# Four units of r: columns two ahead, splits a product earlier, Silu as one pass per row, the fourth unit's sums in memory

## The chip, the cores and the metric

One core of a Trainium2 chip runs the whole program. The metric is the device time of one execution in microseconds (us); lower is better. The engines are named as in the profile: PE (TensorE, the matmuls), ACT (ScalarE), DVE (VectorE), POOL (GpSimd), and SP (SyncE), which issues the DMAs. Each engine takes its instructions in the order in which they were written into its queue.

## The reference

One layer of an encoder trunk over 1024 tokens of width 1024, in float32. What matters here, cut:

```python
h = rmsnorm(x, norm_mix)
q, k, v, r, lr_f, lr_b, u, g_a, g_b = split(h @ w_in)
# four heads: a gated linear attention over chunks, forward scan plus backward scan
o = gla_chunked(q, k, v, log_a_f) + flip(gla_chunked(flip(q), flip(k), flip(v), flip(log_a_b)))
o = o * rsqrt(mean(o * o) + EPS) * gla_norm
o = o * silu(r)                       # r: 1024 x 1024, the product h @ w_in[:, r columns]
y_a = o @ w_branch_gla
y_b = pooled(u) @ w_pool_group * pool_scale
x = x + (sigmoid(g_a) * y_a + sigmoid(g_b) * y_b) @ w_out
x = x + (silu(gate) * up) @ w_ffn_out      # gate, up = split(rmsnorm(x) @ w_ffn_in)
return rmsnorm(x, norm_final)
```

## The kernel before, in words

**Numbers and products.** A float32 operand is split into a high and a low part (`split_to`, L200): ACT casts the high part (`wh`, `trh`, `kt`, `p`, L201 or L689), then POOL (for weights, `wl`, L202) or DVE (for activations, `trl` L693, `kt`, `p`) subtracts it from the operand for the low part. A product takes three matmuls: high by high, low by high, high by low. The big projections use a seven-product scheme for a 2 x 2 block of a matrix product: products p = 1 to 7, each of a sum of weight blocks with a sum of blocks of h. Products 1, 2 and 4 take weight blocks as they lie in memory, 3, 5, 6 and 7 take sums of blocks; on the side of h, products 4 to 7 take sums ("feature sums", held in memory as `f_out`, loaded by `load_sums` into `trl`, cast by `cast_sum` into `trh`, and made low by `low_sum`).

**Units of r.** The columns of r fall into four units of 256 (u = 0 to 3; TRIO = 3). Units 0 to 2 are the r stage: 21 products in the order `R_PRODUCTS` by unit, with weights that are loaded by `r_load` (tiles `rr`, from `w_in` for p = 1, 2, 4 and from `r_out` for the sums) and split by `r_split`. `r_out` is filled early: `r_jobs` (L642) loads a unit's two column tiles (`rraw`), has POOL form four sums of them (L742), and stores them (L723). These jobs run beside the attention of the second and third heads, one step at a time (`beside`, L713; `prepare_beside`), and `finish_beside` ends what is left in head 3's projection. Unit 3 is handled as unit 0 of the stage after (`gunits`, `gate_runs`, `Gates`): its sums are formed by DVE (`fs`, L1189) from two loaded column tiles (`fraw`), ahead of use by `Ahead`.

**What runs beside it.** `attention(h)` is a generator that is advanced in small steps between the matmuls of whatever PE projects (`pump`, L166, takes the time passed; `soon` puts a step off by a delay). In the r stage that is the attention of head 3. Its state goes through `advance` (L972): PE makes kv, DVE the new state `st`, ACT two scaled copies, `sf` or `sb` for PE and `so` for the next state; forward chunks use sf, backward chunks sb. `scores` (L992) masks by a DVE copy (L1002), and splits the result into p for PE. At the head's end the output is normed and turned, and stored to `o_out` (L563).

**Order around the change.** `project_qk(3)` (L852) calls, ahead of k's products, `finish_beside`, the load of the feature sums for p = 5 and the loads of the first four r weights; after each half of k it splits one. In the r stage each product n loads weight n + 5 and splits n + 3, and then runs the steps of `r_events` (L1337): loads and casts of feature sums two or three products ahead of use, the loads of `o_out` (`ol`), and `gate_row`. `r_evict` (L1323) takes a bank out of PSUM: the first product of a quarter is copied, later ones are added by DVE, and the last one goes through Silu on ACT, in halves of 512 columns. `gate_row` multiplies a row of r by o.

Of the kernel before, what the change touches and what calls it, by code (L numbers as in the profile page):

```python
# [10 lines left out]
F32 = mybir.dt.float32  # L11
# [43 lines left out]
def kernel(  # L55
# [583 lines left out]
    TRIO = KT // 2 - 1  # L639
    r_out = [{p: dram.tile([P, 4, P], F32, name=f"r_out{u}_{p}") for p in (3, 5, 6, 7)} for u in range(TRIO)]  # L640

    def r_jobs(u):  # L642
        raw = [slot(F32, (KT, P), "rraw")[:, :, :] for _ in range(2)]
        a11, a12, a21, a22 = (t[:, 4 * j : 4 * j + 4, :] for t in raw for j in range(2))
        yield from loading(
            [w_in[:, c0 : c0 + P].rearrange("(k p) c -> p k c", p=P) for c0 in (R0 + 2 * u * P, R0 + (2 * u + 1) * P)], raw
        )
        for op, dst, a, b, p in (
            (padd, a22, a21, a22, 5), (psub, a21, a11, a21, 7), (psub, a11, a22, a11, 6), (psub, a12, a12, a11, 3)
        ):  # L650
            yield partial(op, dst, a, b), None, r_out[u][p]

# [195 lines left out]

    def r_weight(u, p, k):
        return tuple(t[:, k, :] for t in r_parts[u, p])  # L850

    def project_qk(h, last=False):  # L852
        q = slot(s="q")
        k = slot(s="k")
        for dst, scale in ((q, DK**-0.5), (k, 1.0)):
            final = last and dst is k
            w = take(not final)
            if final:
                value_weights[0].splits(2)
            elif last:  # L860
                value_weights.append(ValueWeights())
            begun = h == HEADS - 1 and dst is k
            if begun:
                finish_beside()
                load_sums(R_PRODUCTS[1])
                for n in range(4):
                    r_load(n)
            for half in range(2):
                ps = feature_major(w, hT, half)
                nc.scalar.activation(dst[:, half, :], ps[:, :], AF.Copy, scale=scale)  # L870
                if begun:
                    r_split(half)
        if begun:
            r_load(4)
            r_split(2)
        qk_heads[h] = q, k

    def attention(h):
# [93 lines left out]
        def advance(old, n, d, kt, dst, ends=False):  # L972

            kv = bank(ps_g, "kv")
            products(kv[:, :DV], tokens((kt[:, 0, :], kt[:, 1, :]), n), value(n))
            new = s1((DV,), "st")[:, :]
            after = factor(n, d, "after")
            if old is None:
                nc.vector.tensor_scalar(new, kv[:, :DV], after, None, op0=ALU.mult)
            else:  # L980
                nc.vector.scalar_tensor_tensor(
                    new, kv[:, :DV], after, old[:, :], op0=ALU.mult, op1=ALU.add
                )
# [5 lines left out]
            nc.scalar.activation(old[:, :], new, AF.Copy, scale=factor(following, d, "whole"))  # L989
            return old  # L990
# [129 lines left out]
        if h == HEADS - 1:  # L1120
            o_heads[h] = o
            norm_and_turn(0)
            norm_and_turn(1)
            return
# [27 lines left out]
    for h in range(HEADS):  # L1152
# [96 lines left out]

    R_RUN = 1, 2, 6, 5, 3, 7, 4  # L1250

    def steps_of(n, last=False):
# [3 lines left out]
    def product(unit, p, ps, right):  # L1256
# [15 lines left out]
    gates_ahead = Ahead(  # L1272
        gunits, [(0, p) for p in R_RUN] + list(chain(*(steps_of(n, n == len(gate_units) - 1) for n in range(1, len(gate_units)))))
    )
# [40 lines left out]
    def gate_row(u, i):  # L1315
        j, row = 2 * u + i, r_rows[u][i]
        for half in range(2):
            dst = row[:, half, :]
            turned_product(dst, ol[u, i][:, half, :], dst)
            gated_o.append((ob_out[j // 4, half][:, j % 4, :], dst))  # L1320
        soon(3, store_gated)

    def r_evict(u, p, ps):  # L1323
# [11 lines left out]
        nc.scalar.activation(dst, ps, AF.Silu)  # L1335

# [4 lines left out]

    for p in R_PRODUCTS:
        if p not in FIRST[:2] and p != 3:
            at = TRIO * R_PRODUCTS.index(p)
            if p != 5:
                event(at - 5, partial(load_sums, p))
            event(at - 3, partial(cast_sum, p, 0))
            event(at - 2, partial(cast_sum, p, 1), partial(low_sum, p, 0))
            event(at - 1, partial(low_sum, p, 1))
# [5 lines left out]
    event(17, partial(load_block_again, 0))  # L1355
    event(18, partial(load_block_again, 1))
    event(16, *[gunits[0].load] * 2)
    event(14, finish_side)
    event(17, gates_ahead.step)
    event(19, gates_ahead.step)  # L1360

    for n, (u, p) in enumerate(r_sequence):
        if n:
            flush()
        r_load(n + 5)
        r_split(n + 3)
        for step in r_events.get(n, ()):
            step()
        if p in (2, 5, 1):
            r_banks[u] = bank(ps_mm)  # L1370
        ps = r_banks[u]
        product(lambda p, k: r_weight(u, p, k), p, ps, right)
        r_evict(u, p, ps[:, :])
    for step in r_events[len(r_sequence)]:
        step()
    sa_out, yb_out = (dram.tile([P, 2, KT, HALF], F32, name=n) for n in ("sa_out", "yb_out"))
# [268 lines left out]
    mm_banks = cycle([ps_mm] * MM_BANKS + [ps_g] * (8 - MM_BANKS))  # L1645
    for _ in range(AHEAD - 2):
        gates_ahead.step()
    zs = {}
    LOADS = 0, 1
    for n, run in enumerate(gate_runs):  # L1650
# [8 lines left out]
        for at, (of, p) in enumerate(run):  # L1659
            if not gates_ahead.step() and at in (5, 7):  # L1660
                line_make()
# [599 lines left out]
```

## Time and profile before

| what | value |
|---|---|
| median of 3 runs | 1386.15 us (1385.58 to 1387.24) |
| the profiled execution | 1387.01 us, span 1385.3 us |
| mean granted clock | 0.995 |
| PE busy | 1355.8 us (98%) |
| ACT, DVE, POOL busy | 653.0, 855.8, 781.0 us |
| head 3's projection and the r stage | about 215 to 360 us of the span |
| the fourth unit | about 361 to 380 us |

Times in rows are microseconds from the start of the span. A row of a timeline is start, duration, engine, line, operation, output from input, and in brackets how long the engine had idled before it and what it waited for. In a row of waits stand the waiting engine and line, what it waited for, total, times and longest. The row of a stretch shows each engine's busy time with its count of instructions, the granted TensorE clock (1.00 is full), the DMA engines' busy share, and GB/s.

### The profile page before, as it was taken

What the parts mean: (1) busy time and instruction counts of PE and PEld (TensorE: products, weight loads), DVE (VectorE), ACT (ScalarE), POOL (GpSimd) and SP (SyncE); (2) the same over time, 40 slices, a digit from 0 to 9 for tenths busy, and PEclk for the clock granted to TensorE, in tenths of its full rate; (3) what the DMA queues carried; (4) which work ended last, traced back from release to release, by engine and by line L of the source; (5) the groups of instructions that cost most, each with busy time, mean ns of one, the idle gap of its engine ahead of it and who ended that gap; (6) DMA issues with size and microseconds to landing.
All of it is one profiled execution on the core that took longest, in us unless ns stands there. A gap on an engine that the chain in (4) does not pass through costs nothing. (4 is left out here: it accounts for less than half of the span.)

```text
span 1385.3 us, 17868 instructions
## 1 busy us (share of the span) xinstructions
PE 1355.8 (98%) x6226; PEld 1123.8 (81%) x6226; DVE 855.8 (62%) x1059; ACT 653.0 (47%) x1189; POOL 781.0 (56%) x582
## 2 busy tenths in 40 slices
PE   9999998998899999999999999999999999999998
PEld 7888886877688888888888888888888888888886
DVE  6965565566635786687884856555655556343375
ACT  7366665675434444554356533333333334444353
POOL 3332926152578555568665176666766667545454
PEclk9999999999999999999999999999999999999999
DMA  7343626263868668996616355555444447975551
GB/s 225 121 156 93 193 82 189 75 179 101 296 204 268 192 217 268 354 402 226 209 62 228 122 183 175 175 175 174 146 139 144 144 150 266 384 295 188 173 213 76
DMA packets 184971, 265.35 MB, mean 192 GB/s; under 512 B 12168, under 2 KB 106416, under 8 KB 184880
## 3 DMA queue, kind: packets, MB, share of 16 engines
q1 hardware_dynamic: 184736, 263.95, 57.0%
q8 instruction: 49, 0.80, 0.2%
q14 instruction: 42, 0.34, 0.1%
q10 hardware_dynamic: 144, 0.26, 0.0%
HBM read 176.87 MB, written 87.29 MB: 191 GB/s over the span
## 5 line engine op out<-in xcount | busy, mean ns | idle before, releaser
L202 POOL TENSOR_TENSOR wl<-fs,wh 128x512 fp32r<-128x512 f32 x124 | 170.9, 1383 | 163.9 <-ACT wh L201 107.9
L273 PE MATMUL ps<-gh,wh 128*128 128x512 f32 x616 | 240.5, 390 | 0.0
L273 PE MATMUL ps<-gl,wh 128*128 128x512 f32 x616 | 239.8, 389 | 0.3 <-DVE gl L1819 0.3
L273 PE MATMUL ps<-gh,wl 128*128 128x512 f32 x616 | 239.7, 389 | 0.0
L202 POOL TENSOR_TENSOR wl<-fraw,wh 128x512 fp32r<-128x512 f32 x93 | 133.1, 1431 | 64.5 <-ACT wh L201 61.7
L202 POOL TENSOR_TENSOR ol<-gor,oh 128x1024 fp32r<-128x1024 f32 (+1 forms) x42 | 101.4, 2417 | 86.0 <-ACT oh L201 71.2
L273 PEld LDWEIGHTS ps<-gl,wh 128*128 128x128 f32 x616 | 115.7, 188 | 24.5 <-DVE gl L1819 0.7
L273 PEld LDWEIGHTS ps<-gh,wl 128*128 128x128 f32 x616 | 115.6, 188 | 24.1
L273 PEld LDWEIGHTS ps<-gh,wh 128*128 128x128 f32 x616 | 115.7, 188 | 24.0 <-DVE sums L1985 0.2
L273 PE MATMUL ps<-hh,wl 128*128 128x512 f32 x296 | 116.6, 394 | 6.7 <-POOL wl L202 6.7
L273 PE MATMUL ps<-hh,wh 128*128 128x512 f32 x296 | 120.8, 408 | 1.7 <-ACT wh L201 1.1
L273 PE MATMUL ps<-oh,oh 128*128 128x512 f32 x308 | 119.8, 389 | 0.0
L273 PE MATMUL ps<-ol,oh 128*128 128x512 f32 x308 | 119.8, 389 | 0.0
L273 PE MATMUL ps<-oh,ol 128*128 128x512 f32 x308 | 119.8, 389 | 0.0
L273 PE MATMUL ps<-hl,wh 128*128 128x512 f32 x296 | 116.3, 393 | 1.1 <-DMA hl<-h_out 1.1
L202 POOL TENSOR_TENSOR wl<-wraw,wh 128x512 fp32r<-128x512 f32 x56 | 91.8, 1669 | 44.3 <-ACT wh L201 37.5
L202 DVE TENSOR_TENSOR ol<-wor,oh 128x1024 fp32r<-128x1024 f32 (+1 forms) x42 | 61.8, 1483 | 66.8 <-ACT oh L201 54.3
L201 ACT CAST wh<-fs 128x512 fp32r<-128x512 f32 x124 | 76.1, 615 | 30.4 <-DVE fs L1189 29.4
L273 PE MATMUL ps<-trl,wh 128*128 128x512 f32 x224 | 87.6, 391 | 2.7 <-DVE trl L693 2.7
L273 PE MATMUL ps<-trh,wh 128*128 128x512 f32 x224 | 88.9, 397 | 1.1 <-ACT ga L1603 1.1
L273 PE MATMUL ps<-trh,wl 128*128 128x512 f32 x224 | 87.3, 390 | 0.0
L273 PEld LDWEIGHTS ps<-hh,wl 128*128 128x128 f32 x296 | 56.1, 189 | 19.5 <-POOL wl L202 7.6
(286 smaller groups left out, 3111.3 us busy)
## 6 DMA issues: line engine op xcount, KB each, us to landing
fraw<-in_w_ffn_in_dram SPq DMA_DIRECT2D x44, 512.0 KB, 6.1
gor<-g_out SPq DMA_DIRECT2D x35, 512.0 KB, 6.0
fraw<-in_w_in_dram SPq DMA_DIRECT2D x22, 512.0 KB, 6.8
g_out<-s SPq DMA_DIRECT2D x44, 256.0 KB, 2.3
wor<-t_out SPq DMA_DIRECT2D x20, 512.0 KB, 4.2
g_out<-g SPq DMA_DIRECT2D x33, 256.0 KB, 2.6
x<-in_x_dram SPq DMA_DIRECT2D x16, 512.0 KB, 4.4
wor<-in_w_ffn_out_dram SPq DMA_DIRECT2D x15, 512.0 KB, 7.0
```

What stands on the lines that cost most here:

```text
L201: nc.scalar.copy(hi, src)
L202: eng.tensor_tensor(lo, src, as_f32(hi), op=ALU.subtract)
L273: nc.tensor.matmul(ps, a[i], b[j], start=first and n == 0, stop=last and n == 2, skip_group_check=onto)
```

## The change

It has these parts:

1. `r_jobs` becomes one generator for all four units: the columns of units 0 and 1 are loaded at its start, those of unit u + 2 after the sums of unit u. The fourth unit gets sums in `r_out` like the others (four POOL sums and four stores more, and loads from `r_out` in place of DVE's sums).
2. The r weights of all four units are one sequence, and `r_step` splits one and loads the one three further on. Head 3's projection makes two such steps right after `finish_beside`, ahead of k's products, and one after each half; the feature sums for p = 5 are split there too, after a delay.
3. Backward chunks copy `so` ahead of `sb`.
4. `r_evict` does no Silu; `gate_row` does it over a whole row of 1024 and then multiplies each half, a little later each. The events move: rows are gated at products 16 to 23 (before 14 to 21), and feature sums are loaded and cast earlier. The last head's norm and turn are put off by `soon`.
5. The fourth unit uses `RUnit` and runs 1, 6, 5, 3, 2, 7, 4 (before 1, 2, 6, 5, 3, 7, 4).

```diff
+        for u in range(2):
+            yield partial(load_columns, u), None, None
+        yield None, None, None
+        for u in range(TRIO + 1):
+            a11, a12, a21, a22 = (t[:, 4 * j : 4 * j + 4, :] for t in raws[u] for j in range(2))
+            for op, dst, a, b, p in (
+                (padd, a22, a21, a22, 5), (psub, a21, a11, a21, 7), (psub, a11, a22, a11, 6), (psub, a12, a12, a11, 3)
+            ):
+                yield partial(op, dst, a, b), None, r_out[u][p]
+            if u + 2 <= TRIO:
+                yield partial(load_columns, u + 2), None, None
...
-    r_sequence = [(u, p) for p in R_PRODUCTS for u in range(TRIO)]
+    R_RUN = 1, 6, 5, 3, 2, 7, 4
+    r_products = [(u, p) for p in R_PRODUCTS for u in range(TRIO)]
+    r_sequence = r_products + [(TRIO, p) for p in R_RUN]
...
+    def r_step():
+        n = next(r_steps, None)
+        if n is not None:
+            r_split(n)
+            r_load(n + 3)
+        return n is not None
...
                 finish_beside()
                 load_sums(R_PRODUCTS[1])
-                for n in range(4):
+                for n in range(3):
                     r_load(n)
+                for _ in range(2):
+                    r_step()
             for half in range(2):
                 ps = feature_major(w, hT, half)
                 nc.scalar.activation(dst[:, half, :], ps[:, :], AF.Copy, scale=scale)
                 if begun:
-                    r_split(half)
-        if begun:
-            r_load(4)
-            r_split(2)
+                    r_step()
+                    soon(1, partial(cast_sum, R_PRODUCTS[1], half))
+                    soon(3, partial(low_sum, R_PRODUCTS[1], half))
...
-            nc.scalar.activation(dst, new, AF.Copy, scale=factor(following, d, "before"))
-            if ends:
-                return None
-            old = s1((DV,), "so")
-            nc.scalar.activation(old[:, :], new, AF.Copy, scale=factor(following, d, "whole"))
+            old = None if ends else s1((DV,), "so")
+            scaled_to = [(dst, "before")] + [(old, "whole")] * (not ends)
+            for to, which in reversed(scaled_to) if d else scaled_to:
+                nc.scalar.activation(to[:, :], new, AF.Copy, scale=factor(following, d, which))
             return old
...
-            prepare_beside(map(r_jobs, range(TRIO)), 2)
+            prepare_beside([r_jobs()], 2)
...
-    gunits = [Unit(w_in, cols) for cols in gate_units]
+    gunits = [RUnit(TRIO)] + [Unit(w_in, cols) for cols in gate_units[1:]]
...
     def gate_row(u, i):
         j, row = 2 * u + i, r_rows[u][i]
-        for half in range(2):
+        nc.scalar.activation(row[:, :, :], row[:, :, :], AF.Silu)
+
+        def multiply(half):
             dst = row[:, half, :]
             turned_product(dst, ol[u, i][:, half, :], dst)
             gated_o.append((ob_out[j // 4, half][:, j % 4, :], dst))
-        soon(3, store_gated)
+
+        soon(2, partial(multiply, 0))
+        soon(3, partial(multiply, 1))
+        soon(5, store_gated)
...
-        if p in (2, 5, 3):
+        if p in (1, 6, 7):
+            add(dst, ps, dst)
+        else:
             nc.scalar.copy(dst, ps)
-            return
-        if p != 4:
-            add(dst, ps, dst)
-            ps = dst
-        nc.scalar.activation(dst, ps, AF.Silu)
...
+    for p, loaded_at, cast_at, low_at in ((6, 3, (5, 6), (7, 8)), (7, 8, (12, 12), (13, 13)), (4, 13, (15, 16), (16, 16))):
+        event(loaded_at, partial(load_sums, p))
...
     for u in range(TRIO):
-        event(11 + u, partial(load_ol, u, 0))
-        event(14 + u, partial(gate_row, u, 0))
-        event(15 + u, partial(load_ol, u, 1))
-        event(19 + u, partial(gate_row, u, 1))
+        event(14 + u, partial(load_ol, u, 0))
+        event(16 + u, partial(gate_row, u, 0))
+        event(18 + u, partial(load_ol, u, 1))
+        event(21 + u, partial(gate_row, u, 1))
```

Three places show how instructions move. The first is POOL in front of head 3's first q weight. `rraw` are the columns of r and their sums, `qe` and `fac` belong to head 2's attention, and the last row, `wl` from `raw`, is the weight. Of before, from the first sum of unit 1:

```order
L742 TENSOR_TENSOR rraw_2239<-rraw_2239 128x512
L742 TENSOR_TENSOR rraw_2239<-rraw_2238,rraw_2239 128x512
L950 TENSOR_TENSOR qe_2278<-qe_2278,q_1467 128x512
L951 TENSOR_TENSOR fac_2279<-fac_2279 128x4
L742 TENSOR_TENSOR rraw_2238<-rraw_2239,rraw_2238 128x512
L742 TENSOR_TENSOR rraw_2238<-rraw_2238 128x512
L950 TENSOR_TENSOR qe_2312<-qe_2312,q_1467 128x512
L951 TENSOR_TENSOR fac_2313<-fac_2313 128x4
L202 TENSOR_TENSOR wl_2353<-raw_2227,wh_2352 128x512
```

The same place in the new kernel, from the first `qe` on; unit 1's four sums stand ahead of it, and the rraw rows here are unit 2's:

```order
L978 TENSOR_TENSOR qe_2288<-qe_2288,q_1471 128x512
L979 TENSOR_TENSOR fac_2289<-fac_2289 128x4
L752 TENSOR_TENSOR rraw_2248<-rraw_2248 128x512
L752 TENSOR_TENSOR rraw_2248<-rraw_2247,rraw_2248 128x512
L978 TENSOR_TENSOR qe_2327<-qe_2327,q_1471 128x512
L979 TENSOR_TENSOR fac_2328<-fac_2328 128x4
L752 TENSOR_TENSOR rraw_2247<-rraw_2248,rraw_2247 128x512
L202 TENSOR_TENSOR wl_2365<-raw_2235,wh_2364 128x512
```

Ahead of the weight stood four sums of unit 1 with two qe; now three of unit 2 with two qe, of which one has moved ahead of the first sum.

The second is ACT at the end of q of head 3, up to the first forward state `sf`. `rr` are the first r weights. Of before:

```order
L985 ACTIVATE sb_2427<-st_2534,fac_2313 128x256
L201 CAST p_2554<-sc_2545 128x512
L870 ACTIVATE q_2414<-ps_2525 128x512
L985 ACTIVATE sf_2600<-st_2605,fac_2356 128x256
L989 ACTIVATE so_2608<-st_2605,fac_2356 128x256
```

and now:

```order
L1016 ACTIVATE sb_2442<-st_2550,fac_2328 128x256
L201 CAST p_2570<-sc_2561 128x512
L899 ACTIVATE q_2429<-ps_2541 128x512
L201 CAST wh_2601<-rr_2595 128x512
L201 CAST wh_2607<-rr_2597 128x512
L1016 ACTIVATE sf_2626<-st_2631,fac_2368 128x256
```

Two casts of r weights stand between q's eviction and the state copies; before, the first of them stood behind k's evictions.

The third is ACT in the r stage, from the last `kt` of the backward chunks (head 3) to the cast of the masked scores `p`. Of before:

```order
L201 CAST kt_3201<-kp_3196 128x512
L985 ACTIVATE sb_3111<-st_3208,fac_3002 128x256
L989 ACTIVATE so_3211<-st_3208,fac_3002 128x256
L985 ACTIVATE sb_3111<-st_3220,fac_3002 128x256
L1335 ACT_TABLE_LOAD
L1335 ACTIVATE r_2892<-r_2892 128x512
L201 CAST wh_3230<-rr_3126 128x512
L689 CAST trh_3234<-trl_3084 128x1024
L201 CAST p_3255<-sc_3246 128x512
```

and now:

```order
L201 CAST kt_3233<-kp_3228 128x512
L1016 ACTIVATE so_3242<-st_3240,fac_3030 128x256
L1016 ACTIVATE sb_3140<-st_3240,fac_3030 128x256
L1016 ACTIVATE sb_3140<-st_3252,fac_3030 128x256
L201 CAST wh_3259<-rr_3113 128x512
L201 CAST p_3279<-sc_3270 128x512
```

The table load, the Silu of a half row and the cast of a feature sum (`trh`) are no longer ahead of p; so stands ahead of sb.

More of the change, by code (lines that the diff above doesn't have):

```diff
@@ L639, with r_jobs, load_columns @@
     TRIO = KT // 2 - 1
[L640 to L651, printed above, removed]
+    r_out = [{p: dram.tile([P, 4, P], F32, name=f"r_out{u}_{p}") for p in (3, 5, 6, 7)} for u in range(TRIO + 1)]
+    def r_jobs():
+        raws = []
+        def load_columns(u):
+            raws.append([slot(F32, (KT, P), "rraw")[:, :, :] for _ in range(2)])
+            for i, t in enumerate(raws[-1]):
+                c0 = R0 + (2 * u + i) * P
+                nc.sync.dma_start(t, w_in[:, c0 : c0 + P].rearrange("(k p) c -> p k c", p=P))
+        for u in range(2):
[9 more added lines that the diff above has]
+                yield partial(load_columns, u + 2), None, None
     right = {}
@@ L1121, in attention @@
             o_heads[h] = o
-            norm_and_turn(0)
-            norm_and_turn(1)
+            for part in range(2):
+                soon(3 + part, partial(norm_and_turn, part))
             return
@@ L1272 @@
     gates_ahead = Ahead(
-        gunits, [(0, p) for p in R_RUN] + list(chain(*(steps_of(n, n == len(gate_units) - 1) for n in range(1, len(gate_units)))))
+        gunits, chain(*(steps_of(n, n == len(gate_units) - 1) for n in range(1, len(gate_units))))
     )
@@ L1371 @@
         ps = r_banks[u]
-        product(lambda p, k: r_weight(u, p, k), p, ps, right)
+        product(RUnit(u), p, ps, right)
         r_evict(u, p, ps[:, :])
-    for step in r_events[len(r_sequence)]:
-        step()
     sa_out, yb_out = (dram.tile([P, 2, KT, HALF], F32, name=n) for n in ("sa_out", "yb_out"))
@@ L1659 @@
         for at, (of, p) in enumerate(run):
-            if not gates_ahead.step() and at in (5, 7):
+            if n == 0:
+                r_event(len(r_products) + at)
+            if not r_step() and not gates_ahead.step() and at in (5, 7):
                 line_make()
```

43 lines of the change are left out of this document (19 added, 24 removed).

## The prediction

> **What bounds the kernel now.** I read the page first, then the waits of PE, then busy time per stretch of 10 us, and last the timelines around each wait. The page's head gives the span and the engines.
>
> ```profile
> span 1385.3 us, 17868 instructions
> PE 1355.8 (98%) x6226; PEld 1123.8 (81%) x6226; DVE 855.8 (62%) x1059; ACT 653.0 (47%) x1189; POOL 781.0 (56%) x582
> ```
>
> TensorE is busy for 98% of the span. The change leaves the number and kind of its matmuls alone, so all it can win is the idle time of PE, 1385.3 - 1355.8 = 29.5 us, and the stretches in which the clock is low after an idle time. The waits of PE in the part that the change touches (215 to 385 us: head 3's projection, the r products, the fourth unit) are these; the columns are total, times and longest.
>
> ```profile
> PE ps L273 <- POOL wl L202: 6.7, 2, 6.1
> PE op L273 <- ACT p L201: 4.9, 1, 4.9
> PE ps L273 <- DVE trl L693: 2.7, 3, 1.3
> PE ps L273 <- ACT ga L1603: 1.7, 2, 1.1
> PE ps L273 <- ACT wh L201: 1.1, 1, 1.1
> PE ps L273 <- DMA hl<-h_out: 1.1, 2, 0.8
> PE kv L273 <- DVE kt L202: 0.4, 1, 0.4
> ```
>
> They sum to 18.6 us: one wait of 6.1 us for q weights, one of 4.9 us for the masked scores p, and ten small ones. The stretches show the same two holes, and the clock (the third number from the end).
>
> ```profile
> core 0: us, PE busy (x) PEld busy (x) DVE busy (x) ACT busy (x) POOL busy (x), PEclk, DMA share, GB/s
> 220.00:230.00 10.00, 3.94 (x13) 3.00 (x13) 4.00 (x7) 2.33 (x6) 9.92 (x11) 0.68 0.84 237
> 270.00:280.00 10.00, 8.31 (x35) 6.21 (x35) 4.40 (x7) 9.97 (x18) 4.84 (x4) 1.00 0.28 63
> 310.00:320.00 10.00, 5.11 (x20) 4.02 (x19) 6.45 (x10) 7.20 (x12) 2.38 (x2) 0.79 0.55 170
> 320.00:330.00 10.00, 10.00 (x57) 8.92 (x57) 4.25 (x8) 6.03 (x16) 1.46 (x2) 0.87 0.10 26
> ```
>
> The granted clock falls to 0.68 and 0.79 beside the two long waits and stays 1.00 beside the short ones. So the stage is bound by TensorE, with a dozen places where one operand is late.
>
> **The q weights (part 1 of the change).** Timelines of POOL, SP and PE:
>
> ```profile
> 217.00 1.30 POOL L742 TENSOR_TENSOR rraw<-rraw 128x512 f32<-128x512 f32 x1 [14.57 <-DMA rraw<-in_w_in_dram]
> 225.89 1.26 POOL L202 TENSOR_TENSOR wl<-raw,wh 128x512 fp32r<-128x512 f32 x1
> 195.68 11.15 SPq L563 DMA_DIRECT2D o_out<-ot  x8
> 209.52 1.94 SPq L597 DMA_DIRECT2D rraw<-in_w_in_dram  x2
> 220.52 0.40 PE L273 MATMUL ps<-hh,wh 128*128 128x512 f32 x1
> 220.76 0.39 PE L273 MATMUL ps<-hl,wh 128*128 128x512 f32 x1
> 227.21 0.79 PE L273 MATMUL ps<-hh,wl 128*128 128x512 f32 x1 [6.06 <-POOL wl L202]
> 227.80 0.63 PE L273 MATMUL ps<-hh,wh 128*128 128x512 f32 x1
> 228.22 0.63 PE L273 MATMUL ps<-hl,wh 128*128 128x512 f32 x1
> ```
>
> POOL stood 14.57 us for unit 1's columns, which SP issued only at 209.52 because it had stood at the o_out stores; then it had four sums, two qe and two fac before the weight PE wanted, whose end is 225.89 + 1.26 = 227.15. In the new order unit 1's columns are issued ahead of those stores, and its sums run in POOL's idle time. But POOL then has two sums of unit 2 ahead of the second qe, and unit 2's columns sit where unit 1's sat on SP. So I keep 217.0 for their landing: the wait moves one unit on. After it stand three sums, one qe and one fac (in the order shown with the change) and then the weight: five operations of 1.3 us and a fac of about 0.2, end at about 223.6. PE resumes 3.6 us earlier, with 2.5 us of stall left (221.2 to 223.6). After the stall, matmuls start 0.42 apart (227.80, 228.22) instead of about 0.23 (220.52, 220.76), until about 230.5: 3.3 us at about half speed lose 1.5. A stall of 2.5 lies between the 1.3 that kept the clock and the 4.9 that lost it; I credit 1.0 of the 1.5. The Trainium skill ("TensorE: Matmul & The Clock Gate", What's actually happening) says that the array falls cold after an idle window of about 3.4 us; by that the whole 1.5 would come back. Gain 4.6 us, from 0 (columns land 3.6 later) to 7.5 (they land early, no stall).
>
> **The early splits (a new wait).** ACT now has two casts of r weights right behind q's last eviction and ahead of the state sf (they read the rr tiles). They wait for loads that SP issues behind the stores of the last sum and two feature sum loads.
>
> ```profile
> 241.79 2.19 SPq L839 DMA_DIRECT2D rr<-in_w_in_dram  x3
> rr<-in_w_in_dram SPq DMA_DIRECT2D x6, 256.0 KB, 6.2
> 248.17 0.59 PE L1097 MATMUL op<-sf,qe 128*128 128x256 f32 x2
> ```
>
> POOL's remaining work to the last sum is unchanged in amount, so it and the loads behind it move about 3 us earlier: rr issued at 238.8, landing (median 6.2 in the fourth column of the DMA view) at 245.0, two casts of 0.6 each to 246.2, sf, a copy of half a us, ends at 246.7. PE, 3.6 us early, wants sf at 248.17 - 3.6 = 244.6. New stall 2.1, I take 2.0; 0 if the loads land in 3.5 us, up to 4 if they gain nothing on before's issue time. Queued behind the casts are so, the eviction of op and kt, so the state chain moves with it.
>
> **The first r products and turned sums.** These are the three waits for trl and those for wh and for the second wl.
>
> ```profile
> 353.03 0.39 PE L273 MATMUL ps<-trh,wh 128*128 128x512 f32 x1
> 354.74 0.50 PE L273 MATMUL ps<-trl,wh 128*128 128x512 f32 x1 [1.32 <-DVE trl L693]
> ```
>
> With two weights split before k's products, and p=5's sums split inside head 3's projection, nothing is asked of ACT at the first r products that is not long ready; sums of p = 6, 7 and 4 are cast several products ahead instead of two or three. The waits are 1.1 + 0.6 + 2.7 = 4.4 us; start to start each costs a little more (353.03 to 354.74 less a step of 0.23 is 1.48 for a wait of 1.32), so 5.1 us in all. The cover is the queue of four ready weights; if it were gone, these 5.1 stay.
>
> Against that, ACT casts p=6's sums (trh) ahead of kt of head 3's attention, and they wait for a load that SP reaches behind the o_out stores.
>
> ```profile
> 275.29 6.26 SPq L563 DMA_DIRECT2D o_out<-ot  x8
> trl<-f_out SPq DMA_DIRECT2D x4, 512.0 KB, 5.4
> 295.60 0.28 PE L273 MATMUL kv<-vh,kt 128*128 128x256 f32 x1
> ```
>
> The stores end at 281.6 with SP's turn, so the trl loads go out at about 282.5 and land (5.4 in the DMA view of 200 to 300 us) at 288; two casts of 1.1 with evictions between bring kt to about 292, its low part to 293. PE, by then some 4 us early, wants it at 291.4. Charge 1.5 us, between 0 and 3.
>
> **Silu, gating and the backward chain.** The second long wait:
>
> ```profile
> 316.32 0.58 PE L273 MATMUL op<-vh,p 128*128 128x256 f32 x1 [4.89 <-ACT p L201]
> 322.18 0.67 PE L273 MATMUL kv<-vh,kt 128*128 128x256 f32 x1
> 303.96 0.49 DVE L981 SCALAR_TENSOR_TENSOR st<-kv,fac,so 128x256 f32<-128x256 f32 x1 [0.98 <-ACT so L989]
> 312.40 1.28 ACT L1335 ACT_TABLE_LOAD   x1
> 313.70 0.63 ACT L1335 ACTIVATE r<-r 128x512 f32<-128x512 f32 x1
> 314.74 1.04 ACT L689 CAST trh<-trl 128x1024 fp32r<-128x1024 f32 x1
> 315.69 0.58 ACT L201 CAST p<-sc 128x512 fp32r<-128x512 f32 x1
> 312.36 1.22 DVE L693 TENSOR_TENSOR trl<-trl,trh 128x1024 fp32r<-128x1024 f32 x1
> 313.49 0.69 DVE L1002 COPY_PREDICATED sc<-keep,sc 128x512 f32<-128x512 uint8 x1
> ```
>
> Ahead of p, ACT did a table load, a Silu, a weight and a trh, and DVE did a trl ahead of the mask. Now the table load, the Silu, trh and trl are gone from there. DVE's mask can begin at 312.36 in place of 313.49, and p's cast ends at 312.36 + 0.69 + 0.58 = 313.6 in place of 316.27. Besides, copying so ahead of sb takes the 0.4 us of sb out of each step of the state chain (0.98 us of waiting for so in a step); over four such steps 1.7. That puts p at 311.9, against 316.32 - 4.89 = 311.4, when PE began to wait: 0.5 left, or 2.2 without the chain's gain. I take 1.5, since ACT still has a weight ahead of p: gain 3.4. After the long wait matmuls run slow from 316.3 to 322.6, 6.3 us at about 0.53 of the usual rate, 2.9 us lost; a wait of 1.5 should lose none, so 2.9 more. Together 6.3 us, from 2 to 7.8. The Silu's table is still loaded once, later, where PE has weights in hand. The Trainium skill ("ScalarE: Activation LUTs", What ACT_TABLE_LOAD costs) gives about 1.28 us for the load and 1.38 for draining; here the Silu starts 0.02 us after the load ends, so only the 1.28 is seen, and the sum goes by it.
>
> **The fourth unit.** Its sums are done ahead by POOL (four more of 1.3 us, in idle time), go out in four more stores and come back as loads; its p=2 stands fifth, so the h_out waits (1.1 us) should go. The two waits for ga (1.7) are products of one bank in a row; the new order 1, 6, 5, 3, 2, 7, 4 still has two such pairs, so I leave them. Gain 1.1, from -1 (the loads come late) to 2.8.
>
> **Sum.** 4.6 - 2.0 + 5.1 - 1.5 + 6.3 + 1.1 = 13.6 us. The profiled execution took 1387.0 us, 1.7 over its span and 0.9 over the median of the runs, 1386.15. The sum is made against it, giving 1373.4; against the median 1372.5.
>
> **Rivals.** (a) *Every wait goes.* The columns and the casts are in time; then the 18.6 us, the 1.5 and the 2.9 of slow clock are won, 23.0, about 1363. Against it: on SP unit 2's columns stand in unit 1's place. Chance 0.10. (b) *The columns' wait keeps its size*, landing 3.6 us later beside two more columns' transfer (the DMA share is already 0.84): the 4.6 go, the wait of the two casts is then covered (+2.0), and 11.0 us remain, 1375. Chance 0.16. (c) *ACT's waits for loads cost double.* It stands in order at the r weights until 248 (4.0 in place of 2.0) and at trh 1.5 longer, and p is late by 3.5 more, with slow clock: the gain is 13.6 - 7.0 = 6.6, about 1379.5. For it: a landing of 6.2 us was the median, so half of them were later, and a cast stands in front of everything behind it on ACT. Chance 0.17.
>
> (d) *Slower.* The two casts ahead of sf hold up attention and, behind it, k's weights: each us that rr lands after 245 is a us of PE's. It decides from a landing 13.6 us later, at 258.6; landing at 264 gives 19 us more of stall and 1391.5. For that SP would have to stand some 20 us at the fourth unit's columns or stores; before it stood 11.15 us at most there, in stores that now come earlier. Chance 0.04. (e) *Nothing comes of it:* the waits are replaced in kind further on, as the fourth unit's loads arrive late; within 0.2% of before. Chance 0.03.
>
> **How the numbers follow.** My forecast has 0.50. The likeliest gives 1372.5. For the range I leave out (d), (e) and the further half of (a): 1365 to 1380.5. A measurement of this kernel can tell about 0.2%, 2.8 us; faster by more than that are the forecast, (a), (b) and (c) but for a small part of (c): 0.92; within it 0.04, slower 0.04.
>
> **What would show it.** In the new trace: POOL's idle time for rraw moved to the sum of unit 2 and PE's wait for wl at 221 down to about 2.5 us; ACT waiting for DMA rr ahead of sf near 245; no wait for trl, and none for wh at the first r products; p within 2 us of PE and the granted clock near 1.00 where it was 0.79 and 0.87; no wait for h_out. Wrong would make it: PE's wait for wl still 6 us, a wait for sf or kt over 4 us, or p's wait with a low clock still there; then the time lies above 1376.

## The result and the profile after

The changed kernel takes 1376.95 us (median, 1376.78 to 1377.21), the kernel before 1386.7 in the same measurements: a ratio of 0.993, 95% interval 0.9913 to 0.9947, so 9.75 us faster, clear of what the measurement can tell (2.8 us). The forecast was 1372.5, the range 1365 to 1380.5: the direction and the range held, the forecast gain of 13.6 us was too large by 4.

The page of the profiled execution, and PE's waits between 215 and 385 us:

```profile
span 1375.1 us, 17913 instructions
PE 1352.3 (98%) x6226; PEld 1122.9 (82%) x6226; DVE 857.3 (62%) x1055; ACT 654.0 (48%) x1186; POOL 785.3 (57%) x586
```

```profile
PE ps L273 <- POOL wl L202: 4.4, 1, 4.4
PE ps L273 <- ACT r L1362: 2.1, 1, 2.1
PE kv L273 <- DVE kt L202: 1.9, 1, 1.9
PE op L1124 <- ACT sf L1016: 1.9, 2, 1.3
PE ps L273 <- ACT ga L1627: 1.4, 2, 0.7
PE op L273 <- DVE p L202: 0.2, 1, 0.2
```

The waits sum to 11.9 us where they were 18.6. Of the old ones the wait for p is gone (4.9 to 0.2), those for trl, h_out and wh are gone, and the one for wl fell from 6.1 to 4.4. Three are new: for `r`, ACT's copy that frees a bank of PSUM, for `kt` (0.4 before), and for `sf`.

A list of waits doesn't say what a wait was worth. For that I paired the matmuls of the two timelines of PE and took the difference of their starts, the lead of the new kernel:

| place | start before | start now | lead |
|---|---|---|---|
| ahead of head 3's q weights | 200.31 | 200.03 | 0.28 |
| after the wait for wl | 227.21 | 225.26 | 1.95 |
| scores, clock recovered | 238.84 | 237.69 | 1.15 |
| after the first forward state | 248.41 | 248.09 | 0.32 |
| first r products | 275.24 | 272.01 | 3.23 |
| fourth r product | 280.28 | 280.05 | 0.23 |
| after the first trl | 282.68 | 281.68 | 1.00 |
| kv with the second kt | 299.26 | 299.85 | -0.59 |
| behind p, clock recovered | 322.69 | 315.87 | 6.82 |
| after the last states | 337.01 | 331.80 | 5.21 |
| behind p = 4's sums | 355.07 | 346.92 | 8.15 |
| fourth unit's end | 379.69 | 369.46 | 10.23 |

The lead rises and falls: until 300 us the change has won nothing, though it removed the wait for wh and shortened that for wl. The 10.2 us by which the span is shorter are won behind 300 us: p gives 7.4 (with its slow clock), the sums of p = 7 and 4 give 2.9 and the fourth unit 2.1, while 1.6 are given back at the last states.

The granted clock (third number from the end of a row of 10 us) tells the same of p's hole: 0.79 and 0.87 there before, 1.00 now, while 220 to 230 us is still at 0.67.

```profile
220.00:230.00 10.00, 5.62 (x18) 4.44 (x17) 7.15 (x11) 3.61 (x9) 10.00 (x10) 0.67 0.84 271
270.00:280.00 10.00, 7.91 (x35) 6.28 (x34) 7.64 (x11) 9.92 (x18) 2.54 (x2) 1.00 0.33 82
310.00:320.00 10.00, 9.70 (x59) 8.21 (x59) 6.32 (x12) 6.83 (x17) 3.46 (x3) 1.00 0.35 90
320.00:330.00 10.00, 10.00 (x59) 8.92 (x58) 6.78 (x11) 5.75 (x15) 2.70 (x3) 1.00 0.41 133
```

**Where the gains ahead of 300 us went.** POOL's and PE's timelines at the q weights:

```profile
217.80 1.29 POOL L752 TENSOR_TENSOR rraw<-rraw 128x512 f32<-128x512 f32 x1 [4.34 <-DMA rraw<-in_w_in_dram]
223.02 2.19 POOL L202 TENSOR_TENSOR wl<-raw,wh 128x512 fp32r<-128x512 f32 x1
225.26 0.80 PE L273 MATMUL ps<-hh,wl 128*128 128x512 f32 x1 [4.38 <-POOL wl L202]
```

The wait for the columns moved on to unit 2, as forecast: its sum starts at 217.80. The weight then took 2.19 us (1.26 before), so PE resumed at 225.26 and not at 223.6. ACT at the early casts, and PE:

```profile
245.73 0.62 ACT L201 CAST wh<-rr 128x512 fp32r<-128x512 f32 x1 [2.05 <-DMA rr<-in_w_in_dram]
246.66 0.62 ACT L201 CAST wh<-rr 128x512 fp32r<-128x512 f32 x1 [0.30 <-DMA rr<-in_w_in_dram]
247.18 0.50 ACT L1016 ACTIVATE sf<-st,fac 128x256 f32<-128x256 f32 x1
247.74 0.70 PE L1124 MATMUL op<-sf,qe 128*128 128x256 f32 x2 [0.56 <-ACT sf L1016]
```

ACT stands 2.05 and 0.30 us for the loads and the state copy stands behind it. Then the r products, ACT first:

```profile
275.81 1.28 ACT L933 ACT_TABLE_LOAD   x1
277.10 2.05 ACT L933 ACTIVATE z<-z 128x512 f32<-128x512 f32 x4
279.03 0.63 ACT L1362 COPY r<-ps 128x512 f32<-128x512 f32 x1
279.71 0.50 PE L273 MATMUL ps<-trh,wh 128*128 128x512 f32 x1 [2.09 <-ACT r L1362]
```

PE reaches its fourth product with all three banks of the r products in use; the copy that frees one stands behind a table load and four logarithms. Before, the same copy began at 278.71, while PE came late and did not notice. Last, kt, with ACT and DVE ahead of it:

```profile
288.85 1.05 ACT L699 CAST trh<-trl 128x1024 fp32r<-128x1024 f32 x1 [1.06 <-DMA trl<-f_out]
291.31 1.05 ACT L699 CAST trh<-trl 128x1024 fp32r<-128x1024 f32 x1 [0.41 <-DMA trl<-f_out]
297.98 1.22 DVE L703 TENSOR_TENSOR trl<-trl,trh 128x1024 fp32r<-128x1024 f32 x1
299.11 0.68 DVE L202 TENSOR_TENSOR kt<-kp,kt 128x512 fp32r<-128x512 f32 x1
299.85 0.38 PE L273 MATMUL kv<-vh,kt 128*128 128x256 f32 x1 [1.94 <-DVE kt L202]
```

### The profile page after: what moved, and what is told of

The parts are those of the page before. It is cut to its first block, busy times and chain, and to the rows that moved or that the text cites. A ratio compares the mean times of both kernels' runs of the same rounds, so it can differ in the third digit from the quotient of the medians.

```text
span 1375.1 us, 17913 instructions
## 1 busy us (share of the span) xinstructions
PE 1352.3 (98%) x6226; PEld 1122.9 (82%) x6226; DVE 857.3 (62%) x1055; ACT 654.0 (48%) x1186; POOL 785.3 (57%) x586
## 5 line engine op out<-in xcount | busy, mean ns | idle before, releaser
L202 POOL TENSOR_TENSOR wl<-fs,wh 128x512 fp32r<-128x512 f32 x120 | 165.6, 1384 | 156.7 <-ACT wh L201 100.4
L202 POOL TENSOR_TENSOR wl<-fraw,wh 128x512 fp32r<-128x512 f32 x90 | 129.1, 1434 | 62.8 <-ACT wh L201 60.2
L201 ACT CAST oh<-wor 128x1024 fp32r<-128x1024 f32 (+1 forms) x42 | 41.1, 978 | 65.0 <-PE ps L273 25.1
```

The source lines that it names most:

```text
L201: nc.scalar.copy(hi, src)
L202: eng.tensor_tensor(lo, src, as_f32(hi), op=ALU.subtract)
```

## The experiments

Two theories. **S** is the prediction's: each wait is worth its own length, and the terms add. **G** (gates): a chain of ACT or DVE that does not move with PE arrives at some places at its own time, and whatever lead PE has there is handed back. All times below are medians, and "slower" and "faster" are said against 1376.95, the changed kernel, unless another is named.

The kernel before was measured again beside each group of runs: 1386.7 us with the changed kernel, 1387.5 with `x_late`, `x_cols`, `x_dve` and `x_sums`, 1387.82 with `x_so`, `x_silu`, `x_run` and `x_rr`, 1386.6 with the other four. So a difference between two groups is uncertain by about 1 us. Taken over the kernel before of its own group, `x_late` is 2.5 us slower than the changed kernel, `x_so` 3.6, `x_silu` 2.4 and `x_run` 8.6, and `x_sums` is 4.5 faster, `x_rr` 1.9 and `x_cols` 1.7.

**The early splits behind k's evictions** (`x_late`):

```diff
-                for _ in range(2):
-                    r_step()
...
+        if begun:
+            for _ in range(2):
+                r_step()
         qk_heads[h] = q, k
```

> The changed kernel, with the two early splits of r weights put behind k's evictions again (still four weights ahead from then on). Theory G (gates): PE's lead over before is cut at places where ACT or DVE arrive late by a chain of their own, so the early splits only cost: the waits for sf at 247.7 us (0.56 and 0.3 more) go, no wait for wh comes back at the first r products, since PE is held there by ACT's copy of r (2.09 us) anyway; about 0.8 us faster than the changed kernel, 1376. Theory S (the sum of the prediction): the early splits are what removed the waits for wh and wl (1.07 and 0.62 us, in all about 2), so these come back and outweigh the sf waits: about 1 us slower, 1378.

Measured: 1380.28, 3.3 slower. The wait for sf near 248 us is gone, but PE waits for wh and wl:

```profile
274.79 0.50 PE L273 MATMUL ps<-hh,wh 128*128 128x512 f32 x1 [2.19 <-ACT wh L201]
276.15 0.50 PE L273 MATMUL ps<-hh,wl 128*128 128x512 f32 x1 [0.63 <-POOL wl L202]
```

```profile
275.00:280.00 5.00, 4.37 (x12) 3.12 (x12) 1.97 (x3) 4.97 (x9) 5.00 (x4) 0.66 0.40 107
```

The clock fell to 0.66 after waits of 2.19 and 0.63. The early splits pay for themselves, as S says (it expected 1 us), and G was wrong to hold this place for closed: the gate at 280 costs PE 2.1 us at full clock, the missing weights cost more and the clock too.

**The third unit's sums put off** (`x_cols`), on top of `x_late`:

```diff
             if u + 2 <= TRIO:
                 yield partial(load_columns, u + 2), None, None
+            for _ in range(4 * (u == 1)):
+                yield None, None, None
```

> As x_late, and the third unit's sums are put off by four more steps, so that POOL has no sum of it ahead of the first two q weights. Both theories: the wait for wl (4.38 us) goes, with the slow clock behind it (0.8 us). If the columns' wait is the cause, the weight ends near 218 us, ahead of PE's need at 221, and PE's lead at 228 is near 6 us. Theory S: 5 us faster than x_late, near 1371. Theory G: ACT's work after the second head's attention moves with PE, so 3 to 5 of it stay until 280 us, but the loads of turned sums behind the stores don't get earlier, and the waits for kt at 300 us grow: 1 to 3 us faster than x_late. If the slow weight was itself the cause (it took 2.19 us in place of 1.26), the wait stays at 1 us or more.

Measured: 1376.08, 4.2 faster than `x_late`: between S (5) and G (1 to 3), so it settles neither. The wait for the first wl is gone, which shows that sums of unit 2 ahead of the weight were its cause. Of a lead of 6.7 us over the changed kernel, 3.7 was left at 244 us. PE had waited 1.9 us in the second head's attention, and nearly as much went to a clock of 0.80 at 230 to 235 us:

```profile
225.72 0.38 PE L273 MATMUL kv<-vh,kt 128*128 128x256 f32 x1 [0.79 <-DVE kt L202]
228.18 0.36 PE L273 MATMUL kv<-vh,kt 128*128 128x256 f32 x1 [1.14 <-DVE st L1010]
```

**The first copies of r on DVE** (`x_dve`):

```diff
         if p in (1, 6, 7):
             add(dst, ps, dst)
+        elif p == 2:
+            nc.vector.tensor_copy(dst, ps)
         else:
```

> The changed kernel, with the first three copies of r (p = 2) made by DVE in place of ACT. Theory S: the wait for r at 279.7 us (2.09 us) goes and the kernel is 2 us faster, 1375. Theory G: the wait goes, PE's lead at 282 us is about 3 us in place of 1.0, and all of it is handed back at kt at 300 us, whose wait grows from 1.94 to about 4, since ACT stands there at the casts of turned sums that wait for their load (288.9 us) whatever PE does: within 0.5 us of the changed kernel.

Measured: 1377.71, no gain, as G says, though not by its way: the wait for kt did not grow to 4 us, it is 1.96. DVE and PE:

```profile
276.45 2.20 DVE L703 TENSOR_TENSOR trl<-trl,trh 128x1024 fp32r<-128x1024 f32 x1 [2.18 <-ACT trh L699]
278.57 1.27 DVE L1362 COPY r<-ps 128x512 f32<-128x512 f32 x2
279.40 0.47 PE L273 MATMUL ps<-trh,wh 128*128 128x512 f32 x1 [1.15 <-ACT z L933]
```

The copy stands behind a low part of 2.20 us, so the bank is free less than half a us sooner, and the lead over the changed kernel is 0.31 at 280 and 0.02 at 294.

**Sums of p = 6 cast later, p = 7's low parts apart** (`x_sums`):

```diff
-(6, 3, (5, 6), (7, 8)), (7, 8, (12, 12), (13, 13))
+(6, 3, (7, 8), (8, 9)), (7, 8, (12, 12), (13, 14))
```

> The changed kernel, with the casts of p = 6's turned sums two and two products later (7, 8; low parts 8, 9), and the second low part of p = 7 one product later (14). Theory G: ACT no longer stands at the load ahead of qe, z and kt, so kt comes some 3 us earlier: the wait of 1.94 us at 299.9 goes, and with the low part apart the wait of 1.35 us for sf at 331.5 falls under 0.5; 3 us faster, 1374. Theory S': the load was not what held kt but DVE's scan ahead of it; then the kt wait stays over 1.2 us and the kernel gains under 1.5. A wait for trl at 320 to 335 us would show the low part too late.

Measured: 1373.2 (1372.41 to 1376.61), 3.7 faster, as G expected. No wait for kt nor for sf at 331 is left, so the turned sums ahead of kt were what held it. (PE came late to this place here, but `x_rrsums` below, where it did not, has no wait for kt either.) The edit moves casts and low parts together: it does not part ACT's wait for the load (1.06 and 0.41 us) from the casts themselves, nor from the low part of 1.22 us that stood on DVE right ahead of kt. For the wait at 331, the changed kernel has both low parts of p = 7 on DVE in one piece, ahead of a state:

```profile
326.99 3.47 DVE L703 TENSOR_TENSOR trl<-trl,trh 128x1024 fp32r<-128x1024 f32 x2
```

The profiled execution of `x_sums` took 1376.61; in it the first r weights landed late, and PE waited longer for sf.

```profile
247.34 0.62 ACT L201 CAST wh<-rr 128x512 fp32r<-128x512 f32 x1 [3.52 <-DMA rr<-in_w_in_dram]
249.30 0.70 PE L1124 MATMUL op<-sf,qe 128*128 128x256 f32 x2 [1.98 <-ACT sf L1016]
```

**so behind sb again** (`x_so`):

```diff
-            for to, which in reversed(scaled_to) if d else scaled_to:
+            for to, which in scaled_to:
```

> The changed kernel, with sb copied ahead of so again in the backward chunks. If the chain of states bounds p (theory of the prediction), its step is 0.4 us longer from copy to copy, p of the fourth product group arrives 1 to 1.7 us later than in the changed kernel (where PE waited 0.22 us for it at 312.8), so a wait of 1.2 to 1.9 us there, and the time is 1.0 to 1.7 us more: 1378 to 1378.7. If something else holds p (the two casts ahead of it), the time is the same within 0.5 us.

Measured: 1381.64, 4.7 slower, more than expected. PE waits for p as forecast, and a step of the states on DVE takes 1.46 us from start to start in place of 1.06 to 1.13:

```profile
315.85 0.39 PE L273 MATMUL op<-vh,p 128*128 128x256 f32 x1 [1.54 <-ACT p L201]
```

Against the changed kernel the lead falls by 1.64 there, and by 1.6 more at a low clock (0.76 at 315 to 320 us; the leads are -2.13, -3.77, -5.36). The other 2.1 stood already at 250 us, in longer waits for wl (4.98) and sf (1.19); whether those come of the edit, which also touches the second head, or of the execution, one profile does not settle.

**Silu in the evictions again** (`x_silu`): `r_evict` as before the change, no Silu in `gate_row`, the events left as changed.

```diff
-        nc.scalar.activation(row[:, :, :], row[:, :, :], AF.Silu)
...
-        if p in (1, 6, 7):
+        if p in (2, 5, 3):
+            nc.scalar.copy(dst, ps)
+            return
+        if p != 4:
             add(dst, ps, dst)
-        else:
-            nc.scalar.copy(dst, ps)
+            ps = dst
+        nc.scalar.activation(dst, ps, AF.Silu)
```

> The changed kernel, with Silu back in the eviction of each quarter of r (halves of 512, as before) and no Silu in the gating of rows. Theory of the prediction: the table load and a Silu stand ahead of p on ACT again, so p is 1.3 + 0.6 us or more later than in the changed kernel, PE waits about 2 us for it at 313 to 316, the clock stays high or dips a little, and the time is 2 to 4 us more, 1379 to 1381. Rival: the casts of turned sums (trh, trl), which stay moved here, were what made p late before; then p is late by under 1 us and the time within 1 us of the changed kernel.

Measured: 1380.45, 3.5 slower, as expected of the table load.

```profile
311.27 1.28 ACT L1364 ACT_TABLE_LOAD   x1
314.23 0.39 PE L273 MATMUL op<-vh,p 128*128 128x256 f32 x1 [1.74 <-ACT p L201]
```

In the changed kernel the cast of p starts when its mask is done (311.42 and 311.45 us); here it starts 1.7 us after it (311.90 and 313.60), with the table load, a Silu and a weight between. The lead falls by 1.65 at p and by 1.8 more behind it at a low clock (0.66 at 315 to 320 us), which the expectation did not have.

**The fourth unit in the old order** (`x_run`):

```diff
-    R_RUN = 1, 6, 5, 3, 2, 7, 4
+    R_RUN = 1, 2, 6, 5, 3, 7, 4
```

> The changed kernel, with the fourth unit's products in the old order 1, 2, 6, 5, 3, 7, 4 (its sums still come from memory). If the order is what removed the waits for h_out (0.27 and 0.80 us before), p = 2 asks for it some 3 products sooner and about 1 us comes back, 1378; if the earlier place of its loads relative to PE did, nothing changes: within 0.5 us.

Measured: 1386.64, 9.7 slower; next to nothing of the gain is left (ratio to the kernel before 0.9991, interval 0.9982 to 1.0001). Both expectations missed it.

```profile
363.76 0.79 PE L273 MATMUL ps<-hh,wh 128*128 128x512 f32 x1 [6.45 <-DMA hh<-h_out]
365.04 0.79 PE L273 MATMUL ps<-hl,wh 128*128 128x512 f32 x1 [0.49 <-DMA hl<-h_out]
```

```profile
355.52 0.33 SPq L715 DMA_DIRECT2D hh<-h_out  x1
```

```profile
360.00:370.00 10.00, 5.75 (x13) 4.01 (x14) 1.49 (x1) 0.96 (x2) 2.19 (x2) 0.51 1.08 369
```

SP issues the reload of h from 355.52 on; PE has its first part at 363.76, and the DMA view of 340 to 372 us gives 9.0 and 9.6 us as medians to landing, beside a DMA share of 1.08. But p = 2 comes second: PE waits 6.9 us in all and then runs at a clock of 0.51. The change moved that reload three products back (events 20 and 21 in place of 17 and 18); only the new order, with p = 2 fifth, hides it.

**The first r weights ahead of the feature sums** (`x_rr`):

```diff
+                for n in range(3):
+                    r_load(n)
                 finish_beside()
                 load_sums(R_PRODUCTS[1])
-                for n in range(3):
-                    r_load(n)
```

> The changed kernel, with the loads of the first three r weights issued ahead of the feature sums' loads in head 3's projection (and ahead of whatever jobs finish_beside still holds). The wait for sf near 248 us (0.56 and 0.3 us, up to 2 us in other executions) is put down to ACT standing at the two early casts until these loads land; issued about 1 us sooner and with less ahead of them they land 1 to 3 us sooner, and the wait goes: 0.8 to 1.5 us faster, about 1375.8, with less spread. If the landing is set by the stores and loads that share the DMA engines, the casts start where they did (245.7 us) and nothing changes.

Measured: 1376.17, 0.8 faster, as expected, though less than the measurement can tell. The casts begin at once and the wait for sf near 248 us is gone:

```profile
239.18 1.55 SPq L851 DMA_DIRECT2D rr<-in_w_in_dram  x3
243.06 1.13 ACT L201 CAST wh<-rr 128x512 fp32r<-128x512 f32 x2
278.34 0.50 PE L273 MATMUL ps<-trh,wh 128*128 128x512 f32 x1 [2.10 <-ACT r L1362]
```

The loads go out at 239.18 (240.06 in the changed kernel) and are there by 243.06, not at 245.73: at most 3.9 us and not 5.7 to land, with the two larger loads behind them. The lead over the changed kernel is 1.24 at sf and still 1.37 at the fourth r product, where PE waits as long as before (2.10), and the wait for kt is the same too (2.0). So these chains are not fixed in time, as G has it: they move along when PE is earlier ahead of them.

**Together** (`x_rrsums`): the edits of `x_rr` and `x_sums`.

> The changed kernel with the edits of x_rr and x_sums together: the first r weights loaded ahead of the feature sums, p = 6's sums cast two products later, p = 7's low parts apart. The waits they remove lie at different places (sf at 248; kt at 300 and sf at 331), so by theory G as by theory S the gains add: x_rr gained 0.8 us, x_sums 3.7, together 4 to 5: about 1372.3, with less spread than x_sums since the landing of the first r weights is what varied there.

Measured: 1371.61 (1371.15 to 1372.22); ratio to the kernel before 0.9898, interval 0.9883 to 0.9912. It beats both kernels, the changed one by 5.3 us, a little more than expected. PE's fourth r product starts at 279.71 as in the changed kernel, and from there the low part of the first kt comes 3.0 us earlier (290.94 for 293.98) and that of the second 4.2 earlier (294.95 for 299.11). Between 215 and 385 us PE waits only for these:

```profile
PE ps L273 <- POOL wl L202: 4.9, 1, 4.9
PE ps L273 <- ACT r L1362: 2.1, 1, 2.1
PE ps L273 <- ACT ga L1627: 1.4, 2, 0.7
```

**With the copies on DVE too** (`x_dve2`).

> x_rrsums with the first three copies of r on DVE. In x_dve that edit gained nothing: DVE made the copy behind a low part of 2.2 us (PE's wait for the bank still 1.15 us), and what was won was gone at kt. With the kt wait out of the way theory G expects about 1 us of the 2.1 to reach the end: 1371.3. Theory D (DVE's own chain of scans is then the bound, and three copies of 0.64 us in it are paid back): the same as x_rrsums or up to 1.5 us slower, with a wait for kt back near 300.

Measured: 1372.33, 0.7 slower than `x_rrsums`: less than the measurement can tell, so the time settles nothing. The traces speak for D, though the wait came elsewhere: PE's wait at the fourth product is 0.9 us shorter (1.17), but DVE makes the second kt 1.5 us later (296.42 for 294.95), and p came late instead of kt.

```profile
310.13 0.38 PE L273 MATMUL op<-vh,p 128*128 128x256 f32 x1 [0.79 <-ACT p L201]
```

**With the third unit's sums put off as well** (`x_best`).

> x_dve2 with the third unit's sums put off (the edit of x_cols), so POOL has the first two q weights ahead of them. In x_cols the wait for wl of 4.4 us went, and of a lead of 6.7 us at 230 some 3.7 was left at 244 (0.8 and 1.1 us were handed back to kt and st of the second head's attention, the rest to a low clock). Theory G and S: 3 to 4 us faster than x_dve2, about 1368. Rival: the sums that are put off delay the loads behind them, the early casts make sf wait 2 us or more at 244 to 248, and the gain is under 1.5 us.

Measured: 1374.42, 2.1 slower than `x_dve2`. The rival was right:

```profile
226.05 15.84 SPq L735 DMA_DIRECT2D r_out<-rraw  x6
241.99 1.74 SPq L853 DMA_DIRECT2D rr<-in_w_in_dram  x3
245.15 0.62 ACT L201 CAST wh<-rr 128x512 fp32r<-128x512 f32 x1 [5.39 <-DMA rr<-in_w_in_dram]
247.53 1.22 PE L1126 MATMUL op<-sf,qe 128*128 128x256 f32 x2 [4.29 <-ACT sf L1018]
```

SP stood 15.84 us at stores of sums that POOL had not formed yet; the r weights behind them came at 245, ACT stood 5.39 us at their cast, and PE's lead of 5.4 us over `x_dve2` fell to 0.9 at sf, with a clock of 0.66 at 245 to 255 us.

**Part 1 alone on the kernel before** (`b_cols`): `r_jobs` as in the change, for three units; nothing else.

> The kernel before with part 1 alone for its three units (columns of two units at the start, the third unit's two ahead). The wait for wl falls from 6.06 to about 4.4 us as in the changed kernel, and there are no early casts for sf to wait for. If the changed kernel lost its lead of 1.7 us at 228 to the slow clock and to sf, most of it stays here: 1.2 to 2 us faster than before. If part 1 by itself gains nothing because something up to 280 us takes the lead back, the time is within 0.5 us of before.

Measured: 1386.29, no change (ratio 0.9995, interval 0.9986 to 1.0005). PE's wait for wl is 5.67 us, hardly shorter, so it could win nothing there: neither branch of the expectation, since the wait itself did not fall to 4.4. Here all four sums of unit 2 stand on POOL between the landing of the columns (218.46 us) and the weight, in the changed kernel three; so this run does not tell what part 1 is worth in the changed kernel's order.

## Why the prediction was right, and where it was off

The direction and its main reason were right: the stage is bound by PE, which loses time at single late operands, and the largest of them, p, came in time. The time lies just above 1376, though none of the signs named for that came: no wait for wl of 6 us, none for sf or kt over 4, and no wait for p with a low clock.

1. **q weights, forecast 4.6, measured 0.9** (lead 0.28 to 1.15). The mechanism was right: the wait for columns moved to unit 2. Two sizes were off. PE resumed 1.7 us later than worked out, since the columns landed 0.8 later and the weight took 2.19 us; and the stall of 4.4 us did not spare the clock, with 0.8 of the lead lost behind it. `b_cols`, part 1 for three units on the kernel before, gained nothing.
2. **Early splits, forecast -2.0, measured -0.8.** The place and the time were nearly as worked out (sf ready at 247.7 against 246.7); PE came later, so it waited less. Terms 1 and 2 together: forecast 2.6, measured 0.04.
3. **First products and turned sums, forecast 5.1.** This term failed in part: "nothing is asked of ACT at the first r products that is not long ready" overlooked ACT's copy of r, which frees the bank for the fourth product. The waits for wh and wl were worth 2.9 us at 275 us, and 3.0 of it was handed back at 280. The sums of p = 5 gave 0.8, those of p = 7 and 4 gave 2.9: 3.6 in all. For these last two the reason given was wrong: only the sums of p = 6 are cast several products earlier than before, those of p = 7 and 4 by at most one, and `x_sums` makes the second low part of p = 7 as late as before without a wait for trl. What ended these two waits is not shown.
4. **kt, forecast -1.5, measured -1.6.** `x_sums` shows that the turned sums of p = 6 are the cause, as forecast. The forecast had only ACT in it, with its casts and the load they wait for; of the 4.2 us by which `x_rrsums` has the second kt earlier, 3.0 are there at the first kt and 1.2 are the low part on DVE.
5. **p, forecast 6.3, measured 7.4.** `x_so` and `x_silu` show that the order of the copies and the Silu's place are each worth about 1.6 us at p and as much again in slow clock: with either undone PE waits 1.5 to 1.7 us. The forecast had p 1.5 late; it was 0.2. The two make 3.3 of the 4.7 us by which the wait shrank, if they add; the casts and low parts that no longer stand ahead of p may have the rest, but no run undoes them.
6. **The last states, not forecast, -1.6.** Two low parts of p = 7 (3.47 us together) stood ahead of a state on DVE; `x_sums` took them apart and the wait went.
7. **Fourth unit, forecast 1.1, measured 2.1.** Here the working was right by luck: the cover, p = 2 standing fifth, was named, but not what it costs if it is gone. `x_run` prices that at some 9 us. The waits that went there (h_out 1.1, and ga from 1.7 to 1.4) are 1.4 us; the other 0.7 is not traced.

In sum 0.9 - 0.8 - 0.1 + 0.8 - 1.6 + 7.4 - 1.6 + 2.9 + 2.1 = 10.0, against 10.2 us of span. Of the rivals, (b) came nearest in time, with its wait at 4.4 and not at 6; (c)'s doubled waits did not come in the changed kernel, but `x_best` met the first of them.

The theories: neither holds alone. S failed at 280 and for `x_dve`, `x_dve2` and `x_best`; G failed for `x_late`, and for `x_rr`, whose lead passed both gates. What agrees with these runs is narrower: a wait that is removed is worth its length up to the next place where PE meets a chain on another engine that has not moved with it, so its worth is read there and not at the wait. A delay goes the same way: `x_silu` and `x_run` each lost about 1.6 us to a slow clock at 280 to 285 us and had 1.4 and 1.1 of it back at kt, whose wait fell from 1.94 to 0.51 and 0.85.

## What to carry to other kernels

Follow the lead, matmul by matmul, and not the list of waits: a wait that vanishes may be handed back at the next operand that comes from a chain which did not move, here a PSUM bank freed by a copy in ACT's queue. An operation that waits for a DMA costs everything behind it on its engine; issue its load ahead of the stores and larger loads, or place it where nothing urgent follows. When a change both delays a load and reorders its use, price each half without the other: together they looked like 2 us, apart one of them cost some 9.

## What the runs showed of the hardware

The clock did not follow the length of a wait alone. In seven executions PE waits 2.09 or 2.10 us for the bank of the fourth r product, at a time between 278.3 and 282.9 us. In four of them (the changed kernel, `x_so`, `x_rr`, `x_rrsums`) the clock stayed 1.00 behind it, in the row of 280 to 285 us. In three it fell: to 0.66 in that row in `x_silu` and `x_run`, and in `x_sums` slow matmuls began 1.6 us after PE had resumed:

```profile
282.86 0.50 PE L273 MATMUL ps<-trh,wh 128*128 128x512 f32 x1 [2.09 <-ACT r L1362]
284.43 0.63 PE L273 MATMUL ps<-trh,wh 128*128 128x512 f32 x1
284.86 0.63 PE L273 MATMUL ps<-trl,wh 128*128 128x512 f32 x1
```

The step there is 0.43 us for 0.23. The Trainium skill ("TensorE: Matmul & The Clock Gate", What's actually happening) tells of a free-running window of about 3.4 us; that the same wait falls differently agrees with a window whose phase is not tied to the wait, but a wait shorter than the window being followed by the slow clock does not agree with needing a whole idle window, unless short gaps around it count too. So here a short wait cost up to about twice its length (`x_so`: 1.54 us of wait and 1.6 more at a low clock), and the wait alone did not tell whether it would.

Two more: in `x_run` the reload of h took 9.0 to 9.6 us to land at a DMA share above 1.0, where the medians of the stores and other loads in that stretch are 4.8 to 5.2; and POOL's split of one weight took 1.26 or 2.19 us, with DVE busy for 4.00 of 10 us beside the first and 7.15 beside the second (a cause that is only argued).
